# Later result stores, an earlier embedding load, two additions on VectorE and another order of weight pieces in the last stage of a hybrid decoder layer

## The chip, the cores and the metric

The kernel runs on one core of a Trainium2 chip. Five engines work side by side, each with its own instruction stream: TensorE (PE in the profile; PEld are its weight loads), VectorE (DVE), ScalarE (ACT), GpSimd (POOL) and SyncE (SP). SP and ACT issue the DMAs of this kernel; "SPq" and "ACTq" mark such an issue. An engine takes its instructions in order, so an instruction that waits holds up all that stand behind it. The metric is the device time of one execution, in microseconds; less is better.

## The reference

One layer of a decoder, in float32, for 2048 prompt tokens and 64 sample tokens of width 1024:

```python
proj = xn @ w_in + b_in
...
y_a = (o * jax.nn.silu(za)) @ w_br_a
...
y_b = (cv * jax.nn.silu(zb)) @ w_br_b
merged = jax.nn.sigmoid(ma) * y_a + jax.nn.sigmoid(mb) * y_b
h = h + merged @ w_o
gate = jax.nn.sigmoid(_rmsnorm(h, norm_ple) @ w_ple_gate)
h = h + gate * (p_l @ w_ple)
...
y_prompt = _rmsnorm(hp, norm_final)
```

The recurrence behind `o` and the convolution behind `cv` stand ahead of the part that is changed. Only the last four statements matter here.

## The kernel before

Stages 1 and 2 (projections, recurrence, convolution, both branches, `merged`) take the first 2320 us or so of the profiled execution and write `merged` to DRAM as `mg_dr`. The change is all in stage 3, the last 490 us.

Every float32 operand of a product is split into a high part (a ScalarE copy that rounds) and a low part (what VectorE or GpSimd then subtracts), and a product is the sum of three TensorE products (high by high, high by low, low by high). Stage 3 takes 256 rows at a time, a *pair* of two 128-row blocks, r = 0 and 1. A pair's 256x1024 by 1024x1024 product is done with seven products of half size in place of eight; each is twelve matmuls into one PSUM tile of 128x512. Left operands are quarters of the input (`a11`, `a12`, `a22`) or sums of quarters (`s1` to `s4`, made on GpSimd at L1281, tile `sf`). Their splits are L1288 (ScalarE) and L1289 (VectorE), tiles `l_a` and `l_s`. Right operands are quarters of the weight (`b11`, `b12`, `b21`, `b22`) or their differences (`t1` to `t4`, in DRAM as `ts_dr`).

Sixteen stages of the loop run one after the other, each with seven products i = 0 to 6. Pairs 0 to 7 are the **first pass**: `h = x + merged @ w_o`. After products 0, 1 and 3 the method `more` adds a running sum to a half row block of `h` (GpSimd, L1331), `close` adds a product from PSUM (VectorE, L1335) and squares it (ScalarE, L1383), `scale` stores `h` to `h_dr` (L1346) and scales it by its norm, and `turn` transposes it into `t_dr` (L1398 to L1403). Pairs 8 to 15 are the **gate pass**: the same seven products on `t_dr` with `w_ple_gate`, plus four small products `pp` (L1428) of the embeddings with `w_ple`. The embeddings `p` are loaded (L1300) and transposed (`turn_p`: tile `pt`, L1415; split at L1417 and L1418 into `x1h` and `x1l`). `gate_sum` (L1360, L1361) and `gate_use` (L1366, L1367) put the gate on; `finish` scales by the final norm (VectorE, L1376) and stores the result from ScalarE's queue (L1377).

The order is written out by hand. The loop issues product i of pair n, then the pair's own VectorE and ScalarE work, then `prepare` (sums and splits for the next pair), and then what `at_step(n, i, fn)` has put behind that product. `finish(1)` of a pair comes after its product 6, `finish(0)` after product 0 of the next pair. Row tiles `h` have three buffers, so that the load of a later block (L1294, SP's queue) waits for the store of an earlier one. The gate pass needs other right operands than the first pass. Sixteen 256 KB pieces of them go during pairs 7 and 8 through three buffers (`bwr`, L1605; splits at L1608 and L1609), `t1` and `t4` come whole (1 MB each, L1639, tile `x0l`, splits at L1645 and L1646), and `w_ple` comes in four pieces during pair 5. At the start of stage 3 the pieces of `b22` (for the last product of pair 0) take the same way.

Sample rows are a small extra product in pairs 3 and 11.

Of the kernel before, what the change touches and what calls it, by code (L numbers as in the profile page):

```python
# [86 lines left out]
def f32(ap):  # L87
    return ap.bitcast(F32)
# [3 lines left out]
def tile_hybrid_step(  # L92
# [1152 lines left out]
    class Pair:  # L1245
# [81 lines left out]
            nc.scalar.activation(out=self.u["p1"], in_=self.ps[0], func=AF.Copy)  # L1327


        def more(self, r, e, t):  # L1330
            nc.gpsimd.tensor_tensor(out=self.part(r, e), in0=self.part(r, e), in1=t, op=ALU.add)  # L1331

        def close(self, r, e, d):
            h = self.part(r, e)
# [35 lines left out]
        def finish(self, r):  # L1370
            b = 2 * self.i + r
            rs = rstd(self.ss[r], P)
            for e in range(2) if (self.i, r) == (7, 0) else (None,):
                c = slice(0, D) if e is None else slice(G * e, G * (e + 1))
                h = self.h[r][:, c]
                nc.vector.scalar_tensor_tensor(out=h, in0=h, scalar=rs, in1=fin["n"][:, c], op0=ALU.mult, op1=ALU.mult)  # L1376
                nc.scalar.dma_start(out=y_p[0, b * P:(b + 1) * P, c], in_=h)  # L1377

    def square(h, out, junk=None):
        n = h.shape[0]  # L1380
# [51 lines left out]
    class Sample:  # L1432
# [72 lines left out]
        def finish(self):  # L1505
            rs = rstd(self.ss, NS)
            nc.vector.scalar_tensor_tensor(
                out=self.h[0:NS], in0=self.h[0:NS], scalar=rs, in1=fin["n"][0:NS], op0=ALU.mult, op1=ALU.mult)
            nc.scalar.dma_start(out=y_s2, in_=self.h[0:NS])

    pairs = [[Pair(i, g) for i in range(8)] for g in range(2)]
    samples = [Sample(g) for g in range(2)]
# [116 lines left out]
    def right_load(w, op):  # L1629

        right_new(op)
        lo = right[op][1]
        if op in QUARTERS:
            r, c = QUARTERS[op]
            src = (w_o, w_ple_gate)[w][0][G * r:G * (r + 1), G * c:G * (c + 1)]
        else:
            r0 = (4 * w + int(op[1]) - 1) * G
            src = ts_dr[r0:r0 + G]
        nc.sync.dma_start(out=f32(lo), in_=src.rearrange("(k p) c -> p k c", p=P))  # L1639

    def right_split(op):
        hi, lo = right[op]
# [17 lines left out]
    def first_pass(q, i):  # L1660
        if i == 0:
            q.keep_p1()
            q.more(0, 0, q.u["p1"])
        elif i == 1:
            q.more(0, 1, q.sum_u(1, "p1", "u2"))
        elif i == 2:
            q.close(0, 0, 2)
        elif i == 3:
            t = q.sum_u(3, "u2", "u3")
            q.more(1, 1, t)  # L1670
            q.more(1, 0, t)
        elif i == 4:
            q.close(1, 1, 4)
            h = q.part(0, 1)
            nc.vector.tensor_tensor(out=h, in0=q.ps[4], in1=h, op=ALU.add)
        elif i == 5:
            q.close(1, 0, 5)
        else:
            q.scale(1)
            q.close(0, 1, 6)  # L1680
# [28 lines left out]
    for n, q in enumerate(stages):  # L1709
        nxt = stages[n + 1] if n < 15 else None  # L1710
        if n < 14:
            at_step(n, 6, stages[n + 2].load_raw)
        if nxt:
            at_step(n + 1, 1, lambda q=nxt: q.split("s4"))
            at_step(n, 3, lambda q=nxt: q.load_h(1))
            at_step(n, 6, lambda q=nxt: q.load_h(0))
        if n < 8:
            at_step(n + 1, 1, lambda q=q: q.turn(1))
            at_step(n + 1, 3, lambda q=q: q.turn(0))
        else:  # L1720
            at_step(n - 1, 4, q.load_p)
            at_step(n, 0, lambda q=q: q.turn_p(0))
            at_step(n, 1, lambda q=q: q.turn_p(1))
            if n < 15:
                at_step(n + 1, 0, lambda q=q: q.finish(0))
# [15 lines left out]
            at_step(7, i + 1, lambda op=op, k=k: piece_split(op, k))  # L1741
    for i, op in ((5, "t1"), (5, "t4")):
        at_step(7, i, lambda op=op: right_load(1, op))
    for i, op in ((7, "t1"), (8, "t4")):
        at_step(7, i, lambda op=op: right_split(op))
    for i, fn in ((6, lambda: b22_load(1, 0, 1, 2)), (7, lambda: b22_split(0)), (7, lambda: b22_load(1, 3)),
                  (8, lambda: b22_split(1, 2)), (8, lambda: b22_split(3))):
        at_step(7, i, fn)
    for k in range(2):
        for e in range(2):  # L1750
            c, i = slice(G * e, G * (e + 1)), 2 * k + e
            at_step(5, i, lambda k=k, c=c, i=i: late_load(("p", i), w_ple[0][P * k:P * (k + 1), c]))
            at_step(5, i + 3, lambda k=k, c=c, i=i: late_split(("p", i), wph[:, k, c], wpl[:, k, c]))
    fin = {}

    def load_fin():
# [2 lines left out]

    at_step(8, 0, load_fin)  # L1760

    stages[1].load_raw()
    b22_load(0, 0, 1, 2)
    stages[0].load_h(1)
    stages[0].load_h(0)
    stages[0].split("s1")
# [2 lines left out]
    stages[0].add("s4")  # L1769
    stages[0].split("a22")  # L1770
    at_step(0, 0, lambda: stages[0].split("s4"))
    at_step(0, 3, lambda: b22_split(0, 1, 2))
    at_step(0, 3, lambda: b22_load(0, 3))
    at_step(0, 4, lambda: b22_split(3))
    for n, q in enumerate(stages):
        smp = samples[n // 8] if n % 8 == 3 else None
        nxt = stages[n + 1] if n < 15 else None
        for i in range(7):
# [4 lines left out]
            if smp and i == 5:  # L1783
                smp.split()
                nxt.split("s2")
            elif nxt:
                prepare(nxt, i)
            if q.gate:
                second_use(q, i)
# [3 lines left out]
                smp.ph = turn_ple(smp.p, NS, 0)  # L1793
            for fn in extra.get(7 * n + i, ()):
                fn()
        if smp:
            for e in range(2):
                (smp.gated if smp.gate else smp.out_proj)(e)
# [3 lines left out]
            else:  # L1802
                at_step(n + 1, 3, smp.scale)
                at_step(n + 1, 5, smp.turn)
    stages[15].finish(0)


_INS = ['x_prompt', 'x_sample', 'state_hgrn', 'state_conv', 'p_prompt', 'p_sample', 'lb_param', 'norm_mix', 'w_in',
# [26 lines left out]
```

## Time and profile before

| | us |
|---|---|
| median of three runs | 2815.18 (2815.08 to 2815.82) |
| the profiled execution's own time | 2815.05 |
| its span in the trace | 2813.3 |
| TensorE busy | 2721.9 (97%) |
| VectorE busy | 2049.3 (73%) |
| ScalarE busy | 997.1 (35%) |
| GpSimd busy | 463.6 (16%) |

The span runs from the first to the last instruction of the trace; the 1.75 us between it and the execution's own time lie around it. The busy shares are means over the whole span. The change is in the last sixth of it, so what counts there are the waits of that stretch: which instruction TensorE waited for, for how long, and what that instruction had waited for.

### The profile page before, as it was taken

How to read it: one execution, taken by the hardware profiler on the slowest of the kernel's cores; microseconds unless marked ns; L12 is line 12 of the kernel's file. 1: busy time of each engine (PE TensorE's matmuls, PEld its weight loads, DVE VectorE, ACT ScalarE, POOL GpSimd, SP SyncE). 2: the span in 40 equal slices, each digit the busy share in tenths (PEclk: the TensorE clock that was granted, in tenths of full speed). 3: DMA queues.
4: the chain of work that ended last, by engine and by line, in shares of the span. 5: the costliest groups of instructions: out<-in, count | busy, mean ns of one | idle time of the engine just before them, and what ended most of it. 6: DMA issues, size and time to landing. Idle time of an engine off the chain costs nothing.

```text
span 2813.3 us, 51106 instructions
## 1 busy us (share of the span) xinstructions
PE 2721.9 (97%) x21063; PEld 2335.1 (83%) x21063; DVE 2049.3 (73%) x3308; ACT 997.1 (35%) x2243; POOL 463.6 (16%) x573
## 2 busy tenths in 40 slices
PE   8999999999999999999999999999999999986997
PEld 6888888888888889989989999898898897765776
DVE  6677777876878787777787868789778655455665
ACT  5333333333332432333332333324244324454332
POOL 2000000000000010101011010101155304453221
PEclk9999999999999999999999999999999999998999
DMA  3212223222221422322222322325877785565321
GB/s 123 71 61 83 76 83 98 76 83 65 83 65 56 139 88 75 104 86 92 79 92 82 99 86 80 101 90 182 260 219 244 223 257 188 160 211 187 113 101 71
DMA packets 354162, 333.09 MB, mean 118 GB/s; under 512 B 20794, under 2 KB 286107, under 8 KB 353928
## 3 DMA queue, kind: packets, MB, share of 16 engines
q1 hardware_dynamic: 279120, 224.43, 26.2%
q10 hardware_dynamic: 74536, 105.20, 10.7%
q8 instruction: 165, 2.70, 0.4%
q14 instruction: 69, 0.57, 0.1%
q0 software_dynamic: 272, 0.19, 0.0%
HBM read 224.58 MB, written 105.18 MB: 117 GB/s over the span
## 4 chain that ended last, share of the span: by engine, by line
PE 81%; DVE 6%; ACT 3%; POOL 3%; issue 2%; DMA 2%; ACTq 0%; SPq 0%; POOLq 0%; DVEq 0%
PE mm L1583 69%; PE ps L1312 2%; PE d32p L504 1%; PE ab L512 1%; DVE acc L756 1%; POOL sf L1281 1%; PE o L602 1%; PE kv L575 1%; PE o L604 1%; DVE h L1367 1%; POOL h L1331 1%; PE pp L1428 1%; ACT l_s L1288 1%; DVE h L1376 1%; DMA h_dr<-h 1%
## 5 line engine op out<-in xcount | busy, mean ns | idle before, releaser
L756 DVE SCALAR_TENSOR_TENSOR acc<-u,cw,acc 128x512 f32<-128x512 f32 x960 | 742.9, 774 | 20.7
L1583 PE MATMUL mm<-x1h,whi 128*128 128x320 f32 (+2 forms) x2112 | 706.6, 335 | 0.0
L1583 PE MATMUL mm<-x1h,wlo 128*128 128x320 f32 (+2 forms) x2112 | 689.2, 326 | 0.0
L1583 PE MATMUL mm<-x1l,whi 128*128 128x320 f32 (+2 forms) x2112 | 689.1, 326 | 0.0
L1583 PE MATMUL mm<-x0h,whi 128*128 128x512 f32 (+1 forms) x1416 | 562.5, 397 | 0.0
L1583 PE MATMUL mm<-x0l,whi 128*128 128x512 f32 (+1 forms) x1416 | 551.3, 389 | 2.5 <-DVE x0l L203 2.5
L1583 PE MATMUL mm<-x0h,wlo 128*128 128x512 f32 (+1 forms) x1416 | 551.4, 389 | 0.3 <-DVE wlo L364 0.3
L1583 PEld LDWEIGHTS mm<-x1h,whi 128*128 128x128 f32 x2112 | 398.0, 188 | 30.9 <-issue 1.9
L1583 PEld LDWEIGHTS mm<-x1h,wlo 128*128 128x128 f32 x2112 | 398.2, 189 | 28.2
L1583 PEld LDWEIGHTS mm<-x1l,whi 128*128 128x128 f32 x2112 | 398.0, 188 | 26.2
L364 DVE TENSOR_TENSOR wlo<-raw,whi 128x1024 fp32r<-128x1024 f32 x176 | 218.4, 1241 | 208.7 <-ACT whi L360 202.6
L1583 PEld LDWEIGHTS mm<-x0h,wlo 128*128 128x128 f32 x1416 | 266.2, 188 | 57.6 <-DVE wlo L364 1.2
L1583 PEld LDWEIGHTS mm<-x0h,whi 128*128 128x128 f32 x1416 | 266.8, 188 | 53.7 <-issue 1.2
L1583 PEld LDWEIGHTS mm<-x0l,whi 128*128 128x128 f32 x1416 | 266.7, 188 | 53.7 <-DVE x0l L203 3.2
L613 POOL TENSOR_SCALAR ors<-oss 128x4 f32<-128x4 f32 (+1 forms) x40 | 12.2, 305 | 1341.8 <-ACT on L611 1341.8
L360 ACT ACTIVATE whi<-raw 128x1024 fp32r<-128x1024 f32 x176 | 186.2, 1058 | 101.7 <-DVE mal L951 35.0
L465 DVE TENSOR_TENSOR rp<-rp 128x512 f32<-128x512 f32 (+1 forms) x224 | 156.7, 699 | 9.9 <-DVE lvl L478 0.5
L478 DVE TENSOR_TENSOR lvl<-kq,rp 128x512 f32<-128x512 f32 (+2 forms) x224 | 150.7, 673 | 1.9
L839 ACT ACTIVATE sp<-mm,vcol 128x512 f32<-128x512 f32 (+2 forms) x120 | 73.0, 609 | 127.4 <-PE mm L1583 115.1
L1312 PE MATMUL ps<-r_t,l_s 128*128 128x512 f32 x384 | 106.4, 429 | 6.8 <-ACT l_s L1288 6.8
L1312 PEld LDWEIGHTS ps<-r_t,l_s 128*128 128x128 f32 x384 | 79.1, 210 | 29.2 <-ACT l_s L1288 9.0
L721 ACT ACTIVATE sg<-mm,vcol 128x512 f32<-128x512 f32 (+2 forms) x40 | 24.6, 614 | 203.4 <-PE mm L1583 163.9
(297 smaller groups left out, 3530.2 us busy)
## 6 DMA issues: line engine op xcount, KB each, us to landing
raw<-in_w_in_dram SPq DMA_DIRECT2D x144, 512.0 KB, 3.9
gate<-am_dr SPq DMA_DIRECT2D x24, 512.0 KB, 5.0
xt<-in_x_prompt_dram SPq DMA_DIRECT2D x16, 512.0 KB, 5.0
g_dr<-gst ACTq DMA_DIRECT2D x32, 256.0 KB, 2.9
cv_dr<-acc ACTq DMA_DIRECT2D x32, 256.0 KB, 2.0
ts_dr<-ts ACTq DMA_DIRECT2D x32, 256.0 KB, 4.3
raw<-in_w_br_a_dram SPq DMA_DIRECT2D x16, 512.0 KB, 4.9
raw<-in_w_br_b_dram SPq DMA_DIRECT2D x16, 512.0 KB, 6.5
```

The source lines that it names most:

```text
L360: nc.scalar.activation(out=b.hi, in_=b.raw, func=AF.Copy)
L364: nc.vector.tensor_tensor(out=b.lo, in0=b.raw, in1=f32(b.hi), op=ALU.subtract)
L465: nc.vector.tensor_tensor(out=io, in0=io, in1=tt, op=ALU.mult)
L478: nc.vector.tensor_tensor(out=o, in0=a, in1=b, op=ALU.mult)
L504: nc.tensor.matmul(dst[32 * b:32 * b + 32, c, s:s + 16], lhsT=kk[:, o:o + 32], rhs=lv[:, o:o + 32].rearrange("p (a e i) -> p a e i", e=2, ...
L512: nc.tensor.matmul(self.ab[o:o + h, c, o + h:o + 2 * h], lhsT=lv[:, P * c + o:P * c + o + h], rhs=lv[:, P * c + o + h:P * c + o + 2 * h], ...
L575: nc.tensor.matmul(self.kv[:, c, :], lhsT=self.kt[:, c, :], rhs=self.v[:, c, :], start=True, stop=True)
L602: nc.tensor.matmul(self.o[:, c, :], lhsT=at[:, c, :], rhs=self.v[:, c, :], start=True, stop=last)
L756: nc.vector.scalar_tensor_tensor(out=self.acc, in0=self.u[:, i:i + G], scalar=w, in1=self.acc, op0=ALU.mult, op1=ALU.add)
L839: nc.scalar.activation(out=s[:, 0:n], in_=ps[:, 0:n], func=func, bias=bias(kind, j))
L1312: nc.tensor.matmul(ps, lhsT=a[:, k, :], rhs=b[:, k, :], start=(k == 0 and j == 0), stop=(k == 3 and j == 2))
L1583: nc.tensor.matmul(ps[:, 0:u.n], lhsT=w[:, k, :], rhs=x[:, k, sl], start=(k == 0 and w is u.block.hi and x is xh), stop=(k == KB - 1 and w ...
```

## The change

All edits are in stage 3.

- The stores of `y` are no longer issued where `finish` computes them. They are put into a list and issued two products later (`y_store`, `y_flush`); what is left is issued at the end.
- The embeddings of pair 8, the first of the gate pass, are loaded after product 0 of pair 6 instead of product 4 of pair 7. Later pairs keep their place.
- After product 3 of a first-pass pair, the two additions `more(1, 1)` and `more(1, 0)` go to VectorE instead of GpSimd.
- `t1` and `t4` of the gate weight are loaded from ScalarE's queue instead of SP's, and each is split one product later. The pieces of `b22` of the gate weight are loaded one or two products earlier, their splits are grouped otherwise.
- The pieces of `w_ple` are still loaded in pair 5 (the last one in pair 6), but split in pair 6.
- At the start, the pieces of `b22` are loaded ahead of pair 1's input and split after product 1 instead of 3; the split of pair 1's `a11` moves from product 0 to product 2.

```diff
-        def more(self, r, e, t):
-            nc.gpsimd.tensor_tensor(out=self.part(r, e), in0=self.part(r, e), in1=t, op=ALU.add)
+        def more(self, r, e, t, engine=nc.gpsimd):
+            engine.tensor_tensor(out=self.part(r, e), in0=self.part(r, e), in1=t, op=ALU.add)
...
-                nc.scalar.dma_start(out=y_p[0, b * P:(b + 1) * P, c], in_=h)
+                y_store(y_p[0, b * P:(b + 1) * P, c], h)
+
+    step = [0]
+    due = []
+
+    def y_store(out, in_):
+
+        due.append((step[0] + 2, out, in_))
+
+    def y_flush():
+        while due and due[0][0] <= step[0]:
+            _, out, in_ = due.pop(0)
+            nc.scalar.dma_start(out=out, in_=in_)
...
-        nc.sync.dma_start(out=f32(lo), in_=src.rearrange("(k p) c -> p k c", p=P))
+        nc.scalar.dma_start(out=f32(lo), in_=src.rearrange("(k p) c -> p k c", p=P))
...
-            q.more(1, 1, t)
-            q.more(1, 0, t)
+            q.more(1, 1, t, nc.vector)
+            q.more(1, 0, t, nc.vector)
...
-            at_step(n - 1, 4, q.load_p)
+            at_step(n - 1 if n > 8 else 6, 4 if n > 8 else 0, q.load_p)
...
-    for i, op in ((7, "t1"), (8, "t4")):
+    for i, op in ((8, "t1"), (9, "t4")):
         at_step(7, i, lambda op=op: right_split(op))
-    for i, fn in ((6, lambda: b22_load(1, 0, 1, 2)), (7, lambda: b22_split(0)), (7, lambda: b22_load(1, 3)),
-                  (8, lambda: b22_split(1, 2)), (8, lambda: b22_split(3))):
+    for i, fn in ((5, lambda: b22_load(1, 0, 1)), (6, lambda: b22_load(1, 2)), (7, lambda: b22_split(0, 1)),
+                  (7, lambda: b22_load(1, 3)), (8, lambda: b22_split(2, 3))):
         at_step(7, i, fn)
...
+    for i, (t0, t1) in enumerate(((0, 8), (1, 9), (2, 10), (9, 13))):
+        k, e = i // 2, i % 2
+        c = slice(G * e, G * (e + 1))
+        at_step(5, t0, lambda k=k, c=c, i=i: late_load(("p", i), w_ple[0][P * k:P * (k + 1), c]))
+        at_step(5, t1, lambda k=k, c=c, i=i: late_split(("p", i), wph[:, k, c], wpl[:, k, c]))
...
+    b22_load(0, 0, 1, 2)
     stages[1].load_raw()
-    b22_load(0, 0, 1, 2)
...
-    at_step(0, 3, lambda: b22_split(0, 1, 2))
-    at_step(0, 3, lambda: b22_load(0, 3))
-    at_step(0, 4, lambda: b22_split(3))
+    at_step(0, 1, lambda: b22_split(0, 1, 2))
+    at_step(0, 1, lambda: b22_load(0, 3))
+    at_step(0, 2, lambda: stages[1].split("a11"))
+    at_step(0, 3, lambda: b22_split(3))
...
-            elif nxt:
+            elif nxt and (n or i):
                 prepare(nxt, i)
...
+            y_flush()
+            step[0] += 1
```

ScalarE, from the square after product 5 of pair 14 to the gate of product 2 of pair 15, before. `g,ss<-h` at L1383 is the square, `p` the copy of product 0, `x1h` the splits of the embeddings' transposes, `out_dram` the stores of `y`:

```order
L1383 ACTIVATE g,ss<-h 128x512
L1377 DMA out_dram<-h 128x1024
L1361 ACTIVATE g<-g 128x512
L1288 ACTIVATE l_s_26823<-sf 128x512
L1383 ACTIVATE g,ss<-h 128x512
L1327 ACTIVATE p_26846<-ps 128x512
L1377 DMA out_dram<-h 128x1024
L1417 ACTIVATE x1h<-pt 128x256
L1288 ACTIVATE l_s_26874<-sf 128x512
L1417 ACTIVATE x1h<-pt 128x256
L1361 ACTIVATE g<-g 128x512
```

The same stretch now (the lines of the file have moved by 12: L1389 is the store, L1395 the square, L1429 the split):

```order
L1395 ACTIVATE g,ss<-h 128x512
L1361 ACTIVATE g<-g 128x512
L1288 ACTIVATE l_s_26822<-sf 128x512
L1395 ACTIVATE g,ss<-h 128x512
L1327 ACTIVATE p_26845<-ps 128x512
L1429 ACTIVATE x1h<-pt 128x256
L1288 ACTIVATE l_s_26872<-sf 128x512
L1429 ACTIVATE x1h<-pt 128x256
L1389 DMA out_dram<-h 128x1024
L1361 ACTIVATE g<-g 128x512
L1395 ACTIVATE g,ss<-h 128x512
L1389 DMA out_dram<-h 128x1024
```

Both stores have moved behind both splits; the store of block 1 from ahead of product 6's gate to behind the second split, the store of block 0 behind the next square.

GpSimd in pair 0 of the first pass, from the second `more` on, before and now. `h<-h,u` are the `more` additions, `sf` the sums for the next pair, `rs` the three steps of a norm:

```order
L1331 TENSOR_TENSOR h<-h,u_23431 128x512
L1331 TENSOR_TENSOR h<-h,u_23467 128x512 x2
L1281 TENSOR_TENSOR sf<-mgr 128x512 x2
L1281 TENSOR_TENSOR sf<-sf,mgr 128x512
L1387 TENSOR_TENSOR rs_23545<-ss 128x1
```

```order
L1331 TENSOR_TENSOR h<-h,u_23428 128x512
L1281 TENSOR_TENSOR sf<-mgr 128x512 x2
L1281 TENSOR_TENSOR sf<-sf,mgr 128x512
L1399 TENSOR_TENSOR rs_23545<-ss 128x1
L1400 TENSOR_SCALAR rs_23545<-rs_23545 128x1
```

The two additions are gone from GpSimd; they stand in VectorE's stream right behind the sum `u` of product 3.

ScalarE from product 5 of pair 7 into pair 8, before. `r_t` are pieces of gate weights, `x0l` and `x0h` the parts of `t1` and `t4`, `x1h<-bwr` the pieces of `b22`:

```order
L1608 ACTIVATE r_t_25100<-bwr 128x512 x3
L1346 DMA h_dr<-h 128x1024
L1383 ACTIVATE junk,ss<-h 128x512
L1288 ACTIVATE l_s_25164<-sf 128x512
L1608 ACTIVATE r_t_25100<-bwr 128x512
L1346 DMA h_dr<-h 128x1024
L1327 ACTIVATE p_25203<-ps 128x512
L1288 ACTIVATE l_a_25205<-mgr 128x512
L1417 ACTIVATE x1h<-pt 128x256
L1645 ACTIVATE x0h<-x0l 128x512 x4
L1608 ACTIVATE x1h<-bwr 128x512
```

The same stretch now:

```order
L1620 ACTIVATE r_t_25100<-bwr 128x512 x3
L1651 DMA x0l<-ts_dr 128x4x512 x2
L1346 DMA h_dr<-h 128x1024
L1395 ACTIVATE junk,ss<-h 128x512
L1288 ACTIVATE l_s_25168<-sf 128x512
L1620 ACTIVATE r_t_25100<-bwr 128x512
L1346 DMA h_dr<-h 128x1024
L1327 ACTIVATE p_25203<-ps 128x512
L1288 ACTIVATE l_a_25205<-mgr 128x512
L1429 ACTIVATE x1h<-pt 128x256
L1620 ACTIVATE x1h<-bwr 128x512 x2
```

The two loads `x0l` are new in this stream, ahead of both stores to `h_dr`; the splits of `x0l` have left this place for a later product.

## Rows read from the trace of the kernel before

**Rows 1.** The page: the busy time of each engine in us (share of the span) and its instructions.

```profile
PE 2721.9 (97%) x21063; PEld 2335.1 (83%) x21063; DVE 2049.3 (73%) x3308; ACT 997.1 (35%) x2243; POOL 463.6 (16%) x573
```

**Rows 2.** The waits of TensorE in stage 3 (2320 to 2814 us): the waiting operation, what released it, then us in total, how many times, the longest.

```profile
PE pp L1428 <- ACT x1h L1417: 33.6, 8, 8.8
PE pt L1415 <- DMA p<-in_p_prompt_dram: 8.7, 1, 8.7
PE ps L1312 <- ACT l_s L1288: 6.8, 5, 3.3
PE ps L1312 <- ACT x1h L1608: 2.8, 2, 1.5
```

**Rows 3.** The chain that ended last, at the step from pair 12 to pair 13 of the gate pass: start, length, what.

```profile
2723.32 0.53 ACT l_a L1288
...
2724.48 1.29 DVE h L1376
2725.79 0.34 ACTq L1377
...
2728.28 7.08 PE ps L1312 x24
...
2756.78 1.66 PE pp L1428 x6
```

**Rows 4.** The timelines of PE, DVE and ACT at the same place: start, length, engine, line, operation, tiles, and in brackets the idle time before it and what ended it.

```profile
2726.61 0.50 PE L1428 MATMUL pp<-x1h 128*128 128x512 f32 x1 [3.23 <-ACT x1h L1417]
...
2727.18 0.40 PE L1428 MATMUL pp<-x1h,x1l 128*128 128x512 f32 x1
...
2726.59 0.42 DVE L1418 TENSOR_TENSOR x1l<-pt,x1h 128x256 fp32r<-128x256 f32 x1 [0.83 <-ACT x1h L1417]
...
2731.75 0.69 DVE L1367 TENSOR_TENSOR h<-g,h 128x512 f32<-128x512 f32 x1
...
2726.98 0.38 ACT L1417 ACTIVATE x1h<-pt 128x256 fp32r<-128x256 f32 x1
```

**Rows 5.** Busy time of each engine in two stretches of 30 us of the gate pass, then the granted clock as a share of full speed, the DMA share and GB/s.

```profile
2715.00:2745.00 30.00, 26.77 (x113) 21.48 (x112) 18.64 (x26) 9.98 (x22) 7.38 (x10) 0.94 0.32 114
2745.00:2775.00 30.00, 26.77 (x120) 21.72 (x119) 18.56 (x27) 10.38 (x24) 8.34 (x13) 1.00 0.23 79
```

**Rows 6.** DMA issues from 2716 to 2735 us (first two rows) and from 2535 to 2565 us (the others): count, KB each, median us from issue to landing.

```profile
out_dram<-h ACTq DMA_DIRECT2D x2, 512.0 KB, 2.6
h<-h_dr SPq DMA_DIRECT2D x2, 512.0 KB, 3.3
...
x0l<-ts_dr SPq DMA_DIRECT2D x2, 1024.0 KB, 10.3
mgr<-t_dr SPq DMA_DIRECT2D x4, 512.0 KB, 11.2
...
h<-h_dr SPq DMA_DIRECT2D x2, 512.0 KB, 7.0
```

**Rows 7.** The start of stage 3, timelines of PE (the last product of pair 0, then products 0 and 1 of pair 1) and DVE.

```profile
2341.25 0.50 PE L1312 MATMUL ps<-x1h,l_s 128*128 128x512 f32 x1 [1.50 <-ACT x1h L1608]
2342.66 0.80 PE L1312 MATMUL ps<-x1l,l_s 128*128 128x512 f32 x1 [0.90 <-DVE x1l L1609]
...
2350.38 3.99 PE L1312 MATMUL ps<-r_b,l_a 128*128 128x512 f32 x12
2354.21 1.98 PE L1312 MATMUL ps<-r_t,l_s 128*128 128x512 f32 x8
...
2341.92 4.05 DVE L1609 TENSOR_TENSOR x1l<-bwr,x1h 128x512 fp32r<-128x512 f32 x3
...
2352.50 0.69 DVE L1289 TENSOR_TENSOR l_s<-sf,l_s 128x512 fp32r<-128x512 f32 x1 [2.59 <-ACT l_s L1288]
```

**Rows 8.** The chain that ended last in the first pass, pairs 1 and 2: start, length, what.

```profile
2374.43 2.61 DMA h_dr<-h
...
2388.54 2.54 POOL h L1331 x2
...
2396.58 2.61 DMA h_dr<-h
```

**Rows 9.** Pairs 5 and 6 of the first pass: PE from product 0 of pair 6 on, and DVE on two of the pieces of `w_ple`.

```profile
2471.52 2.88 PE L1312 MATMUL ps<-r_b,l_a 128*128 128x512 f32 x12
2477.74 4.86 PE L1312 MATMUL ps<-r_t,l_s 128*128 128x512 f32 x12 [3.33 <-ACT l_s L1288]
2482.44 1.03 PE L1398 MATMUL pt<-ident,hs 128*128 128x128 f32 x8
2483.23 0.96 PE L1312 MATMUL ps<-r_b,l_a 128*128 128x512 f32 x3
...
2469.93 1.36 DVE L1609 TENSOR_TENSOR x1l<-bwr,x1h 128x512 fp32r<-128x512 f32 x1 [1.81 <-ACT x1h L1608]
...
2473.87 0.68 DVE L1609 TENSOR_TENSOR x1l<-bwr,x1h 128x512 fp32r<-128x512 f32 x1
```

**Rows 10.** From pair 7 to pair 8: the timelines of PE and ACT.

```profile
2533.59 4.66 PE L1312 MATMUL ps<-r_t,l_s 128*128 128x512 f32 x12 [1.58 <-ACT l_s L1288]
2552.59 0.80 PE L1428 MATMUL pp<-x1h 128*128 128x512 f32 x1 [6.20 <-ACT x1h L1417]
...
2551.64 0.63 ACT L1288 ACTIVATE l_a<-mgr 128x512 fp32r<-128x512 f32 x1 [7.80 <-DMA mgr<-t_dr]
```

More of the change, by code (lines that the diff above doesn't have):

```diff
@@ L1508, in finish @@
                 out=self.h[0:NS], in0=self.h[0:NS], scalar=rs, in1=fin["n"][0:NS], op0=ALU.mult, op1=ALU.mult)
-            nc.scalar.dma_start(out=y_s2, in_=self.h[0:NS])
+            y_store(y_s2, self.h[0:NS])
     pairs = [[Pair(i, g) for i in range(8)] for g in range(2)]
@@ L1743, in tile_hybrid_step @@
         at_step(7, i, lambda op=op: right_load(1, op))
-    for i, op in ((7, "t1"), (8, "t4")):
+    for i, op in ((8, "t1"), (9, "t4")):
         at_step(7, i, lambda op=op: right_split(op))
-    for i, fn in ((6, lambda: b22_load(1, 0, 1, 2)), (7, lambda: b22_split(0)), (7, lambda: b22_load(1, 3)),
-                  (8, lambda: b22_split(1, 2)), (8, lambda: b22_split(3))):
+    for i, fn in ((5, lambda: b22_load(1, 0, 1)), (6, lambda: b22_load(1, 2)), (7, lambda: b22_split(0, 1)),
+                  (7, lambda: b22_load(1, 3)), (8, lambda: b22_split(2, 3))):
         at_step(7, i, fn)
[L1749 to L1753, printed above, removed]
+    for i, (t0, t1) in enumerate(((0, 8), (1, 9), (2, 10), (9, 13))):
[3 more added lines that the diff above has]
+        at_step(5, t1, lambda k=k, c=c, i=i: late_split(("p", i), wph[:, k, c], wpl[:, k, c]))
     fin = {}
@@ L1804, in tile_hybrid_step @@
                 at_step(n + 1, 5, smp.turn)
+    step[0] += 9
+    y_flush()
     stages[15].finish(0)
+    step[0] += 9
+    y_flush()
 _INS = ['x_prompt', 'x_sample', 'state_hgrn', 'state_conv', 'p_prompt', 'p_sample', 'lb_param', 'norm_mix', 'w_in',
```

## The prediction

> **What bounds the kernel now.** The page first: TensorE is busy for 97% of the span [rows 1], so a gain must come out of the time in which it stands still or runs slowly. The view of waits, cut to stage 3, says where it stands still [rows 2]: 33.6 us in eight waits for the split `x1h` of the embeddings, 8.7 in one wait for the first load of `p`, 6.8 for operand splits, 2.8 for the splits of `b22`.
>
> The chain of waits shows why the largest recurs [rows 3]. Where one gate pair follows another it runs through VectorE's final scaling (2724.48, 1.29 us), ScalarE's issue of the store (2725.79) and the split `x1h`, and TensorE restarts at 2726.61 after 3.23 us of idleness [rows 4]. The split needs nothing of the scaling. It stands behind the store in ScalarE's stream, and the store waits for the scaled tile. The next such restart is at 2756.78 [rows 3], 30.17 us later.
>
> The idleness costs twice. Twelve matmuls take 2.88 us where nothing slows them [rows 9]; less the 0.40 of one [rows 4] that is 2.48 for eleven starts, 0.226 apart, so 24 need 5.4. Behind the restart 24 take 7.08 [rows 3], 1.6 more. The stretches say what it is: the granted clock is 0.94 from 2715 to 2745, and 1.00 from 2745 to 2775, which holds the restart at 2756.78 [rows 5]. So TensorE falls to the lower of its two levels (1.2 and 2.4 GHz) behind a restart, though not behind each.
>
> In the first pass the chain runs through GpSimd: `more` for 2.54 us, and later the store of `h`, at 2374.43 and again at 2396.58 [rows 8], 22.15 us apart. TensorE needs 84 matmuls at 0.226 (19.0 us) and two groups of transposes (2482.44 to 2483.23 [rows 9], 0.8 each), 20.6 in all. So this loop leads, not TensorE.
>
> **Part 1, the stores of y.** Without the store `x1h` starts when ScalarE is done with `l_a`, 2723.32 + 0.53 = 2723.85 [rows 3], and ends 0.38 later [rows 4]. Two `pp` matmuls can go; the third reads the low part `x1l`, which VectorE makes behind its scaling, and VectorE's order is as before. The scaling ends at 2725.77, `x1l` takes 0.42 [rows 4], so the third matmul comes at about 2726.25 instead of 2727.18: 0.9 gained. TensorE is then idle in two pieces of about 0.9 and 1.5 us instead of one of 3.23. Whether the clock falls after such a pair is not shown in this order. At the start of the stage pieces of 1.50 and 0.90 are followed by a matmul of 0.80 [rows 7], the lower level; behind the restart at 2756.78 nothing fell. I take half of the 1.6, hence 0.9 + 0.9 = 1.8 per restart, and six restarts of this form (pairs 10 to 15): 10.8 us. Bounds: 6 x 0.9 less 6 x 0.4 (below) is 3; 6 x 2.5 and 1 at pair 9 is 16.
>
> The price is the row tile. Block 0 of the next pair is loaded into the tile that block 1's store reads. That store now stands behind the second split, which ends at 2727.36 [rows 4] and some 2 us sooner without the first store, so it goes at 2725.2; it lands 2.6 later, and the load needs 3.3 more [rows 6], so the tile is there at about 2731.2. Its reader L1367 stands at 2731.75 [rows 4], 0.9 earlier now: 2730.85. Queued behind it on VectorE is the pair's next work, which waits for products of TensorE; those cover the 0.4 us, and without that cover it is 0.4 per pair. At the end the last stores leave later: 0.3 us lost.
>
> **Part 2, two additions on VectorE.** GpSimd loses 2.54 us per pair [rows 8]; VectorE gains two additions of 0.69 (like L1367 [rows 4]). Net 1.2 per pair, of the 1.5 that TensorE allows. It counts where the loop leads, in three pairs ahead of pair 3's sample rows: 3.6 us. Bounds 0 and 5 x 1.5 = 7.5.
>
> The row to weigh is a subtraction of the same size, also with two inputs in SBUF: 0.68 at 2473.87, but 1.36 at 2469.93 [rows 9]. A pair that costs 2 x 1.36 leaves no gain against 2.54, which is the lower bound above. The Trainium skill (SBUF — State Buffer, "SBUF: two separate sides") states that VectorE with two inputs in SBUF and GpSimd lock each other out of a shared port pair for a whole instruction. By that rule, if one addition of each two meets a sum of GpSimd, the term is 3 x 0.5 = 1.5 instead of 3.6. The two durations agree with it.
>
> **Part 3, the pieces of w_ple.** Their four splits leave the vector streams of pair 5, behind which TensorE waited 3.33 us and ran 12 matmuls in 4.86 instead of 2.88 [rows 9]: up to 5.3 us. They come back in pair 6 with 4 x 0.68 on VectorE, nearly all on pair 7's chain: 2.5 of wait and 1.4 of lower clock given back. Net 1.4; bounds -1 and 5.
>
> **Part 4, the start.** The last product of pair 0 waits 1.50 and 0.90 for the `b22` splits and runs slowly until 2350.38 [rows 7]. With three splits two products earlier it can begin when the product before it ends (2341.25 - 1.50 = 2339.75) and needs 2.7 us; the fourth piece is still loaded only when a buffer is free, for which I add 2: it ends near 2344.4. Then the vector chain is late next: product 1 of pair 1 needs `l_s`, which VectorE begins at 2352.50. In that chain stood three splits of `b22`, 4.05 us [rows 7]; they go ahead of it, the two new additions (1.4) come in, so 2.6 are gained, and product 1 starts at about 2350.2 instead of 2354.21: 4 us. Bounds 1 (the splits hold up the first closing instead) and 6.
>
> **Part 5, pair 7 to pair 8.** Product 1 of pair 8 starts at 2533.59, released by `l_s` and not by `p` [rows 10]. So the earlier load of `p`, for all its 8.7 us among the waits, gains nothing by itself. What can gain is `mgr`, for which ScalarE waits 7.80 us until 2551.64, with the next `x1h` behind it and TensorE idle for 6.20 [rows 10]. On SP's queue it stood behind 2 x 1024 KB of `t1` and `t4`, and took 11.2 us [rows 6]. Those are on the other queue now. Between 11.2 and the 3.3 of a tile of the same size elsewhere [rows 6] I take the middle, 7.3: some 4 us sooner, to which 1 to 2 of clock come. Against that: the stores to `h_dr` now stand behind `t1` and `t4`, which take 10.3; the loads of `h` and the last pieces of `b22` on SP wait for them, and `t4` is split a product later. I take 2 off, so +3.5, between 8 (all of `mgr`'s 8) and -3 (nothing for `mgr`, and the stores 3 later).
>
> In that stretch a load of `h` takes 7.0 instead of 3.3 [rows 6], so more of one queue is less of the other. The Trainium skill (DMA: Bandwidth & Descriptors, "Queues, rings and completion order") says that an engine takes turns between the rings that have work, packet by packet. By that rule `mgr` would have half of the rate and land about 5 us sooner; no row here shows two full queues.
>
> **The sum.** 10.8 - 0.3 + 3.6 + 1.4 + 4 + 3.5 = 23.0 us off the profiled execution's 2815.05, which is 0.13 below the median of the runs. Forecast: 2792 us.
>
> **Rivals.**
> A, the forecast. Its own range is 2783 to 2802.
> B, order alone: the clock still falls behind each restart, and pair 7 to 8 gains nothing since it is bound by its sixteen pieces. 4 + 3 + 6 x 0.9 = 12.4: 2803. For it: the 0.80 us matmul behind two short pauses [rows 7]. Against it: a stretch without a fall behind 3.23 [rows 5].
> C, all of the clock and more at pair 7 to 8: 4 + 5 + 8 + 6 x 2.5 = 32, and 5 more if `mgr` and part 3 reach their upper bounds: 2778 to 2783. For it, the exception of rows 5; against it, pair 8's two late operands at once.
> D, slower: the row tile. If the load of `h` takes L instead of 3.3 us, it comes L - 2.95 after its reader is ready, and a gate pair takes 30.17 - 0.9 + L - 2.95. With the 7.0 of the crowded stretch [rows 6] a pair is 3.1 longer; seven pairs make 22, against 12.5 gained elsewhere: 2825. It decides from L = 5.6 on. For it: the load now follows right behind a store, with `mgr` close. Against it: the DMA share of the gate pass is 0.23 to 0.32 [rows 5].
> E, no change: VectorE's work from L1367 to the next scaling is the loop, and each matmul that comes sooner waits longer at the next restart. 2812 to 2818. Against it: the chain passes through 24 matmuls of TensorE in each pair [rows 3].
>
> **Chances.** A 0.55, B 0.25, C 0.08, D 0.06, E 0.06. Faster by over 0.2% (5.6 us, about what a measurement of this kernel can tell from no change) are A, B and C, 0.88; E gives 0.06 for the same, D 0.06 for slower. The range that holds the time 8 times in 10 takes A, B and most of C: 2778 to 2808.
>
> **What would show it.** In the changed kernel's waits of TensorE, `pp` on `x1h` should go from 33.6 to under 10, with `x1l` as a new releaser; the gate restarts should lie about 28.4 apart, with a granted clock of 1.00 in half of the stretches. Product 1 of pair 1 should start near 2350, and ScalarE's wait for `mgr` be under 4 us. A clock of 0.94 in every stretch would show B, VectorE waiting at L1367 for the DMA of `h` D, an unchanged 30.17 E. What would make it wrong by most is a new wait in pairs 7 and 8, where sixteen pieces share three buffers and the order of the loads is new.

## The result and the profile after

The changed kernel takes 2790.49 us (median of three runs, 2789.93 to 2794.97) against 2815.18: a ratio of 0.9916 with a 95% interval of 0.9894 to 0.9939, 24.7 us faster. Timed again in five rounds it took 2795.39 (2795.16 to 2797.32) against 2816.29: 0.9929 (0.9915 to 0.9942), 20.9 us. The forecast was 2792.

The waits of TensorE from 2300 us on in the changed kernel, in the columns of [rows 2] (L1440 is `pp`, L1429 and L1430 are the splits of the embeddings; the lines have moved by 12):

```profile
PE ps L1312 <- ACT l_s L1288: 16.5, 3, 11.2
PE pp L1440 <- ACT x1h L1429: 12.9, 8, 4.4
PE pp L1440 <- DVE x1l L1430: 8.9, 7, 1.3
PE ps L1312 <- ACT x0h L1657: 5.6, 1, 5.6
```

`pp` on `x1h` has gone from 33.6 to 12.9 us (the prediction had under 10), and `x1l` is its new second releaser, 1.3 us at each of seven restarts. The wait for `p` has gone, but `l_s` has grown from 6.8 to 16.5, with one piece of 11.2. That is the same stop at product 1 of pair 8 under another name. The 5.6 us for `x0h` (the split of `t4`) are new.

One restart of the gate pass (the place in each pair where TensorE goes on with the first `pp`) on PE, beside which [rows 4] stands for before:

```profile
2607.68 0.50 PE L1440 MATMUL pp<-x1h 128*128 128x512 f32 x1 [0.78 <-ACT x1h L1429]
2608.01 0.40 PE L1440 MATMUL pp<-x1l,x1h 128*128 128x512 f32 x1
2609.66 0.50 PE L1440 MATMUL pp<-x1h,x1l 128*128 128x512 f32 x1 [1.25 <-DVE x1l L1430]
2610.00 0.39 PE L1440 MATMUL pp<-x1h 128*128 128x512 f32 x1
```

The idle time of 3.2 us has become 0.78 and 1.25, as part 1 had it (0.9 and 1.5), and the matmuls behind it run at 0.39, the higher clock. The sections of stage 3 show the clock at large. Before, then after; columns as in [rows 5] (the last three are granted clock, DMA share, GB/s). The first row of each is the first pass from product 1 of pair 1 to product 1 of pair 7, the second pair 7's product 1 to pair 8's, the third from there to product 3 of pair 9, the fourth the gate pass to the last product of pair 15:

```profile
2354.00:2501.00 147.00, 139.07 (x650) 112.99 (x648) 73.17 (x105) 74.10 (x209) 76.94 (x86) 0.99 0.58 183
2501.00:2534.00 33.00, 22.47 (x103) 17.97 (x104) 19.53 (x23) 19.22 (x46) 20.20 (x19) 0.89 0.63 207
2534.00:2598.00 64.00, 43.58 (x161) 33.56 (x161) 37.81 (x48) 28.18 (x65) 22.36 (x25) 0.82 0.51 181
2598.00:2800.00 202.00, 183.38 (x777) 147.68 (x775) 128.75 (x181) 66.91 (x147) 44.42 (x63) 0.96 0.29 101
```

```profile
2348.00:2490.00 142.00, 137.28 (x649) 113.41 (x648) 83.37 (x119) 73.89 (x210) 61.27 (x76) 0.99 0.61 194
2490.00:2523.00 33.00, 21.84 (x103) 17.70 (x103) 22.14 (x26) 18.86 (x46) 17.66 (x16) 0.89 0.59 199
2523.00:2582.00 59.00, 42.14 (x160) 32.44 (x160) 34.07 (x48) 28.00 (x64) 20.84 (x25) 0.85 0.54 187
2582.00:2776.00 194.00, 180.10 (x779) 144.22 (x779) 129.06 (x182) 66.54 (x147) 45.26 (x63) 0.99 0.31 108
```

The same matmuls take 8 us less in the gate pass, at 0.99 instead of 0.96 of the clock. The first pass is 5 us shorter (3 in the second trace of the changed kernel, see below), with VectorE busy for 10 us more and GpSimd for 16 less. Pair 7 to 8 has not moved, and the section behind it is 5 us shorter.

### The profile page after: what moved, and what is told of

Its sections match the earlier page's. It is cut to its first block, busy times and chain, and to the rows that moved or that the text cites. A ratio compares the mean times of both kernels' runs of the same rounds, so it can differ in the third digit from the quotient of the medians.

```text
span 2788.7 us, 51107 instructions
## 1 busy us (share of the span) xinstructions
PE 2709.7 (97%) x21063; PEld 2328.9 (84%) x21063; DVE 2054.8 (74%) x3324; ACT 996.4 (36%) x2243; POOL 440.3 (16%) x557
## 3 DMA queue, kind: packets, MB, share of 16 engines
q1 hardware_dynamic: 278064, 222.33, 26.3%
## 5 line engine op out<-in xcount | busy, mean ns | idle before, releaser
L1595 PEld LDWEIGHTS mm<-x1l,whi 128*128 128x128 f32 x2112 | 397.7, 188 | 26.3
L1312 PE MATMUL ps<-r_t,l_s 128*128 128x512 f32 x384 | 100.1, 411 | 16.5 <-ACT l_s L1288 16.5
```

The source lines that it names most:

```text
L1312: nc.tensor.matmul(ps, lhsT=a[:, k, :], rhs=b[:, k, :], start=(k == 0 and j == 0), stop=(k == 3 and j == 2))
L1595: nc.tensor.matmul(ps[:, 0:u.n], lhsT=w[:, k, :], rhs=x[:, k, sl], start=(k == 0 and w is u.block.hi and x is xh), stop=(k == KB - 1 and w ...
```

## The experiments

All but the first timing of the changed kernel, above, ran in five rounds beside the kernel before, and each left one trace. The table gives the ratio with its interval, and from the PE timeline of each trace the length of five sections of stage 3 in us: **a** from its first product to product 1 of pair 1, **b** to product 1 of pair 7, **c** to product 1 of pair 8, **d** to product 3 of pair 9, **e** to the last product of pair 15.

| kernel | ratio (95%) | a | b | c | d | e |
|---|---|---|---|---|---|---|
| before | 1 | 31.0 | 147.1 | 32.3 | 64.2 | 202.4 |
| changed | 0.9916 (0.9894 to 0.9939) | 25.9 | 142.1 | 32.8 | 59.6 | 193.5 |
| changed, once more | 0.9929 (0.9915 to 0.9942) | 25.8 | 143.8 | 32.5 | 60.6 | 194.5 |
| stores at once | 0.9957 (0.9945 to 0.9970) | 27.0 | 144.2 | 32.9 | 61.5 | 201.8 |
| before, stores later only | 0.9965 (0.9953 to 0.9978) | 29.9 | 149.0 | 32.0 | 61.8 | 193.4 |
| additions on GpSimd | 0.9955 (0.9941 to 0.9969) | 26.5 | 152.0 | 33.1 | 59.8 | 192.7 |
| before, additions on VectorE only | 0.9967 (0.9955 to 0.9980) | 29.6 | 141.7 | 32.1 | 63.1 | 200.8 |
| w_ple as before | 0.9922 (0.9909 to 0.9934) | 25.8 | 143.8 | 32.6 | 59.3 | 192.3 |
| start as before | 0.9926 (0.9913 to 0.9939) | 29.2 | 144.0 | 32.4 | 60.1 | 192.2 |
| t1, t4 on SP's queue | 0.9928 (0.9914 to 0.9942) | 26.1 | 144.4 | 32.3 | 60.8 | 193.9 |
| p late | 0.9926 (0.9914 to 0.9939) | 26.3 | 143.7 | 34.0 | 60.4 | 195.1 |
| stores one product later | 0.9940 (0.9928 to 0.9953) | 26.2 | 144.4 | 32.8 | 59.2 | 195.5 |
| x1l ahead of the scaling | 0.9901 (0.9887 to 0.9915) | 27.0 | 143.7 | 31.9 | 57.7 | 188.3 |
| that, and t4 split earlier | 0.9917 (0.9903 to 0.9930) | 25.5 | 144.9 | 33.6 | 58.2 | 190.5 |

A section's length varies between traces of the same instructions: **e** is 192.2 to 195.1 in the eight traces that share the changed kernel's gate pass (mean 193.4), and 200.8 to 202.4 in the three with the stores at once; **b** is 147.1 and 149.0 in two kernels that are alike there. A difference of 2 us in one section is therefore no finding by itself.

**The stores.** At once again in the changed kernel:

```diff
-        due.append((step[0] + 2, out, in_))
+        nc.scalar.dma_start(out=out, in_=in_)
```

> The changed kernel with the stores of y issued at once again, all else as changed. Theory (the stores ahead of x1h are what made the gate restarts late, and the idle time of 3.2 us is what lowered the clock): the gate pass loses what the traces give it, 9 us from the first restart of pair 9 to the end, so about 2799 to 2801; single idle pieces of about 3.2 us ahead of pp are back, restarts about 30 us apart, and the granted clock falls behind most of them. Rival (the order of the stores is worth only the 0.9 us by which the third pp matmul comes sooner; the rest came from pairs 7 and 8 being out of the way): 6 x 0.9, so about 2796, with the granted clock as in the changed kernel.

Measured 2804.28 us. Section e is back at 201.8 and the clock is back at 0.94 in three of its stretches. In the waits of TensorE `x1h` is back at 27.6 us, and `x1l` is not among them:

```profile
PE pp L1440 <- ACT x1h L1429: 27.6, 8, 5.9
PE ps L1312 <- ACT l_s L1288: 17.1, 5, 11.2
```

```profile
2620.00:2650.00 30.00, 26.81 (x113) 21.55 (x112) 18.92 (x27) 11.22 (x24) 7.63 (x11) 0.94 0.45 145
2680.00:2710.00 30.00, 27.08 (x114) 21.82 (x113) 20.17 (x28) 11.19 (x24) 6.54 (x9) 0.94 0.30 103
2710.00:2740.00 30.00, 26.81 (x114) 21.51 (x113) 18.58 (x26) 10.12 (x22) 7.36 (x10) 0.94 0.32 112
```

Single idle pieces of 2.8 to 3.2 us stand ahead of the six restarts from pair 10 on again, and the clock fell behind four of them. The theory holds, with 3 us more than it had, 1 to 2 of them in section d; the rival's 2796 does not. The kernel before with the later stores alone (`y_store` and `y_flush` as in the change, nothing else):

> The kernel before with only the stores of y two products later. Theory (the parts add up): 9 us less than before, about 2806, all of it behind pair 9's restart. Rival (the gain in the gate pass needs the other edits, since a late pair 8 leaves the weight splits in its way): 4 us or less, 2811 or more.

Measured 2807.16, with e at 193.4, as in the changed kernel: the theory holds here too. The waits of TensorE keep those of before's first pass and of pairs 7 and 8, 8.1 us for `p` among them:

```profile
PE pp L1440 <- ACT x1h L1429: 18.3, 8, 6.9
PE pt L1427 <- DMA p<-in_p_prompt_dram: 8.1, 1, 8.1
PE pp L1440 <- DVE x1l L1430: 7.9, 7, 1.3
```

So the later stores are worth some 8 us in section e, with the other edits and without them.

**The additions.** Back on GpSimd in the changed kernel:

```diff
-            q.more(1, 1, t, nc.vector)
-            q.more(1, 0, t, nc.vector)
+            q.more(1, 1, t)
+            q.more(1, 0, t)
```

> The changed kernel with the two additions back on GpSimd. Theory from the two traces (between product 1 of pair 1 and the sample rows the change gained 1.3 us): 1 to 2 us slower, about 2792. Rival, the term as it stood in the prediction (1.2 us in each of three pairs): 3.6 us slower, about 2794. Second rival (VectorE's additions beside GpSimd's sums cost as much as they free): no change, 2790.5.

Measured 2802.02, beyond every expectation. Section b takes 152.0, 8 to 10 us more than in the changed kernel and 5 more than before: the early start is given back too. PE at product 1 of pairs 6 and 7, and GpSimd's additions in pair 6:

```profile
2476.32 3.30 PE L1312 MATMUL ps<-r_t,l_s 128*128 128x512 f32 x12 [2.53 <-ACT l_s L1288]
2501.69 2.71 PE L1312 MATMUL ps<-r_t,l_s 128*128 128x512 f32 x6 [3.96 <-ACT l_s L1288]
...
2492.55 2.54 POOL L1331 TENSOR_TENSOR h<-h,u 128x512 f32<-128x512 f32 x2 [4.43 <-DMA h<-in_x_prompt_dram]
```

The wait ahead of product 1 of pair 6 is there although no piece of `w_ple` is split in pair 5. (The second row shows the first six of the product's twelve matmuls.) The additions alone on the kernel before, whose pair 5 still has all four splits:

> The kernel before with only the two additions on VectorE. Theory from the run that undid them (its trace ends 11.5 us behind the changed kernel's, 3.5 of them up to the sample rows and 6 more by product 1 of pair 7): the first-pass loop is where the time is, so they are worth 6 to 10 us alone, 2806 to 2810. Rival (they pay only where the w_ple splits have left pair 5 and stand in pair 6; alone it is the 3.6 us of the prediction): about 2812. Second rival (pairs 7 and 8, bound by their weight pieces, take up all of it): 2815.

Measured 2806.81, 9.9 us less than before: the theory holds, and the prediction's 3.6 falls. Section b is 5.4 us shorter: 1.3 of it between product 1 of pair 1 and that of pair 3, 4.0 between those of pairs 5 and 7. The other 4.3 us of this trace lie in the four other sections, at most 1.6 in each. PE at product 1 of pair 6, which [rows 9] has at 2477.74 behind 3.33 us and at the lower clock:

```profile
2473.48 3.30 PE L1312 MATMUL ps<-r_t,l_s 128*128 128x512 f32 x12 [0.41 <-ACT l_s L1288]
```

Twelve matmuls in 3.30 instead of 4.86, behind 0.41: the additions by themselves take that wait away.

**The pieces of w_ple** as before, in the changed kernel:

```diff
-    for i, (t0, t1) in enumerate(((0, 8), (1, 9), (2, 10), (9, 13))):
...
+    for k in range(2):
+        for e in range(2):
+            c, i = slice(G * e, G * (e + 1)), 2 * k + e
+            at_step(5, i, lambda k=k, c=c, i=i: late_load(("p", i), w_ple[0][P * k:P * (k + 1), c]))
+            at_step(5, i + 3, lambda k=k, c=c, i=i: late_split(("p", i), wph[:, k, c], wpl[:, k, c]))
```

> The changed kernel with the pieces of w_ple loaded and split in pair 5 as before. Theory from the traces (5.5 us gained up to pair 6, 2.2 given back at product 1 of pair 7): 3 us slower, about 2794, with a wait of l_s of about 3 us ahead of product 1 of pair 6 and none ahead of that of pair 7. Rival, the term of the prediction: 1.4 us slower. Second rival (pairs 7 and 8 are bound by their sixteen pieces, which take up whatever pair 6 gains): no change.

Measured 2794.57; b is 143.8, as in the second trace of the changed kernel. My theory from the traces was wrong, and no change, the time of the second rival, is what came. PE at product 1 of pairs 6 and 7 in this run, then in the changed kernel's second trace, shows why:

```profile
2470.54 3.30 PE L1312 MATMUL ps<-r_t,l_s 128*128 128x512 f32 x12 [0.58 <-ACT l_s L1288]
2493.12 3.30 PE L1312 MATMUL ps<-r_t,l_s 128*128 128x512 f32 x12 [0.69 <-ACT l_s L1288]
```

```profile
2468.95 2.89 PE L1312 MATMUL ps<-r_t,l_s 128*128 128x512 f32 x12
2492.87 4.36 PE L1312 MATMUL ps<-r_t,l_s 128*128 128x512 f32 x12 [2.94 <-ACT l_s L1288]
```

With the additions on VectorE the splits in pair 5 cost only 0.58 us ahead of pair 6; split in pair 6 they cost 2 us more ahead of pair 7. Between product 1 of pairs 5 and 7 the two orders differ by 0.5 us (44.2 and 44.7).

**The start** as before (`b22` loaded behind pair 1's input and split after product 3, `a11` after product 0):

> The changed kernel with the start of stage 3 as before (loads and splits of b22, split of a11). Theory (with the additions on VectorE TensorE leads in the first pass, so a late start is carried to the end): 3 to 5 us slower, 2794 to 2796. Rival (the vector loop or the weight pieces of pairs 7 and 8 take it up): no change, about 2791.

Measured 2795.91. Section a is 3.4 us longer (29.2 against 25.8), as the theory had it, and b and c + d are as in the changed kernel's second trace, so the start is still late at pair 9. But e, in which nothing differs, is 192.2 against 194.5, and from the first product of stage 3 to the end of the span this trace has 470.8 us, the two of the changed kernel 470.3 and 466.9. The gain is there at its place and is not taken up by the first pass; what it is worth at the end, between 0.5 and 3.9 us, is within the scatter of e and stays open.

**The queue of t1 and t4**, back on SP:

```diff
-        nc.scalar.dma_start(out=f32(lo), in_=src.rearrange("(k p) c -> p k c", p=P))
+        nc.sync.dma_start(out=f32(lo), in_=src.rearrange("(k p) c -> p k c", p=P))
```

> The changed kernel with t1 and t4 loaded from SP's queue again. Theory, the term of the prediction: mgr then lands 4 us or so later, ScalarE waits for it for 8 to 10 us instead of 6.0, and it is 3 us slower, about 2794. Rival (the DMA engines are full in that stretch, so that another queue only changes who is late, and h_dr's stores gain what mgr loses): no change, about 2791.

Measured 2796.87, ratio 0.9928, as the changed kernel's second timing. ScalarE does wait longer for `mgr`, 8.7 us instead of 6.0, the row of this kernel ahead of that of the changed one:

```profile
ACT l_a L1288 <- DMA mgr<-t_dr: 8.7, 1, 8.7
```

```profile
ACT l_a L1288 <- DMA mgr<-t_dr: 6.0, 1, 6.0
```

Yet c and d together take 93.1 against 92.4 and 93.1 in the two traces of the changed kernel. The rows of `h_dr` and `mgr` at the step from pair 7 to 8, of this kernel and then of the changed one (second trace), from issue to landing, say why:

```profile
h_dr<-h ACTq DMA_DIRECT2D x2, 512.0 KB, 8.1
mgr<-t_dr SPq DMA_DIRECT2D x2, 512.0 KB, 12.2
```

```profile
h_dr<-h ACTq DMA_DIRECT2D x2, 512.0 KB, 13.2
mgr<-t_dr SPq DMA_DIRECT2D x2, 512.0 KB, 10.3
```

The DMA share is 0.93 to 0.95 there in both. The rival holds: `mgr` gains 1.9 us by the other queue and the stores to `h_dr` lose 5.1.

**The load of p**, late again:

```diff
-            at_step(n - 1 if n > 8 else 6, 4 if n > 8 else 0, q.load_p)
+            at_step(n - 1, 4, q.load_p)
```

> The changed kernel with the embeddings of pair 8 loaded behind product 4 of pair 7 again. Theory, as in the prediction (product 1 of pair 8 waits for l_s at about 2522.6, 11 us behind the transposes of p): the load may land up to 11 us later at no cost; same time, with the wait split into one for p and one for l_s. Rival (the transposes and their wait are on the path, as the 8.7 us in the waits of the kernel before suggest, and the load again crowds the weight pieces): 2 to 8 us slower.

Measured 2794.42 against 2795.39 for the changed kernel on the same chip. The wait splits in two, as expected:

```profile
PE pt L1427 <- DMA p<-in_p_prompt_dram: 9.6, 1, 9.6
...
PE ps L1312 <- ACT l_s L1288: 7.7, 4, 2.8
```

An entry of 9.6 us in the list of waits was worth nothing that the timing shows. Section c is 1.2 to 1.5 longer here; whether that is the load's doing stays open.

**The changed kernel once more, and stores one product later** (`step[0] + 1` in place of `step[0] + 2`):

> The changed kernel once more, unedited, so that the others are read beside it on the same chip. It should repeat 2790.5 within 2 us. Its trace tells how much of the differences between traces is chance: the start of stage 3 has come between 2321.8 and 2326.6 us in kernels whose code is the same up to there, and the clock behind the sample rows of pair 3 fell in some traces and not in others.

It took 2795.39, not 2790.5, and its gain is 20.9 us instead of 24.7.

> The changed kernel with the stores of y one product later instead of two. Theory (what counts is that no store that waits for the final scaling stands ahead of x1h in ScalarE's stream): block 0's store still stands behind both splits, so the time is the changed kernel's, about 2790.5, and the gaps ahead of the gate restarts are the same 0.8 and 1.25. Rival (the distance itself counts, since a store that is issued sooner crowds the load of the next row tile): 2 to 4 us slower.

Measured 2800.50 (2796.47 to 2800.71). The gaps at the restarts are the same 0.78 and 1.25, e is 1 us longer, of which 0.7 is a wait for the sample rows' embeddings, and the stretch from the first product of stage 3 to the end is 0.8 longer. The 5 us between the medians are not in the traces (the traced execution, 2797.92, is one of the two quick ones of five; the others took 2800.5 to 2800.7), and the intervals of the two ratios overlap. Whether one product costs something stays open.

**Beyond the change.** The split of the embeddings ahead of the scaling:

```diff
-            at_step(n, 0, lambda q=q: q.turn_p(0))
+            extra.setdefault(7 * n, []).insert(0, lambda q=q: q.turn_p(0))
```

> The changed kernel with one more edit: the split of the embeddings is put ahead of the final scaling of the previous pair in VectorE's stream (the transposes of block 0 are placed first behind product 0). Theory (the third pp matmul waits 1.25 us for x1l only because the scaling of 1.28 us stands ahead of it): this idle time goes at seven restarts, 7 to 9 us faster than the changed kernel, about 2782. Rival (VectorE's chain is the loop of the gate pass, and the scaling that moves behind costs as much later in the pair): less than 2 us, about 2790.

Measured 2788.50, the lowest ratio of all, 0.9901. Its interval overlaps those of the changed kernel, so the time alone does not show a gain, but e is 188.3, against 192.2 to 195.5 in every other kernel with later stores (the last one below shares this edit). PE at the same restart as above:

```profile
2609.98 0.50 PE L1440 MATMUL pp<-x1h 128*128 128x512 f32 x1 [0.76 <-ACT x1h L1429]
2610.32 0.40 PE L1440 MATMUL pp<-x1l,x1h 128*128 128x512 f32 x1
2610.77 0.50 PE L1440 MATMUL pp<-x1h,x1l 128*128 128x512 f32 x1
```

The second piece of idle time is gone, and some 5 us of the expected 7 to 9 came of it in section e. At three restarts the wait for `x1h` has grown instead: by 0.6 us at pairs 11 and 15 and by 1.2 at pair 13 (3.46 instead of 2.27). With the split of `t4` one product earlier (`(8, "t4")` in place of `(9, "t4")`) as well:

> The changed kernel with the split of the embeddings ahead of the final scaling and the split of t4 one product earlier (behind product 1 of pair 8, together with t1's). Theory (in the changed kernel TensorE waits 5.6 us in pair 8 because t4's split stands behind a square on ScalarE that waits for the gate): 3 to 5 us faster than with the embeddings' split alone, and 6 to 8 faster than the changed kernel, about 2783 to 2785. Rival (t1's and t4's splits together hold up the gate of product 2, and the wait moves there): the same as with the embeddings' split alone, 2788.

Measured 2792.65, and e is 190.5. The 5.6 us for `x0h` went, and came back as four others on PE (the last was 2.28 with the embeddings' split alone):

```profile
2559.54 0.50 PE L1440 MATMUL pp<-x1h 128*128 128x512 f32 x1 [0.89 <-DVE g L1360]
2562.05 0.50 PE L1440 MATMUL pp<-x1h 128*128 128x512 f32 x1 [0.84 <-DVE g L1366]
2571.64 4.87 PE L1312 MATMUL ps<-r_t,l_s 128*128 128x512 f32 x12 [2.26 <-ACT l_s L1288]
2583.98 0.80 PE L1440 MATMUL pp<-x1h 128*128 128x512 f32 x1 [4.52 <-ACT x1h L1429]
```

The theory does not hold; the wait moves, as the rival had it, and the 4 us above the rival's 2788 are not explained. Pairs 7 to 9 are bound by something that this split does not shorten; what it is was not found.

## Why the prediction was right, and which steps were not

The total came out within 2 us of the first timing and 3.4 of the second, but not by its own terms, and that it did is luck: part 2 measured 6 us more than it had, and what the other parts measured less makes up for it. The two edits that earn it are the stores (9.5 us alone) and the additions (9.9 us alone): 19.4 of the 20.9 to 24.7. Undoing the order of `w_ple`, the start, the queue of `t1` and `t4` or the load of `p`, each alone, gave ratios of 0.9922 to 0.9928, between the changed kernel's own two, 0.9916 and 0.9929. One edit was never undone by itself: the later splits of `t1` and `t4` and the new order of the gate weight's `b22` (pieces 0 and 1 are loaded one product earlier, the other two where they were).

- Part 1, 10.8 us: right in kind, and near in size (8 in section e, 9.5 alone). Of its two halves the clock did better than taken: at the five restarts with idle pieces of at most 0.8 and 1.35 the clock stayed at the higher level; it fell at the two with 3.19 and 2.27 ahead of 1.25. The restarts of pairs 10 and 11 lie 27.6 us apart (2609.66 to 2637.22), those of pairs 13 and 14, with the lower clock between them, 29.2 (2706.02 to 2735.22). The other traces bear this out, though not without exception. From pair 10 on the clock fell behind 13 of 18 restarts in the three kernels with the stores at once, and behind 9 of 54 in the nine traces with later stores and the old split order: six at pair 13, where `x1h` was 2.2 to 2.6 us late, and three at pair 12 behind pieces of only 0.5 and 1.25, such as this one with the additions on GpSimd (twelve matmuls in 4.14 us; they take 2.9 at the higher clock):

```profile
2689.68 0.50 PE L1440 MATMUL pp<-x1h,x1l 128*128 128x512 f32 x1 [1.25 <-DVE x1l L1430]
...
2691.08 4.14 PE L1312 MATMUL ps<-r_t,l_s 128*128 128x512 f32 x12
```

  Short pieces made a fall rarer and did not rule it out. With the stores at once and no fall pairs 10 and 11 lie 28.5 us apart, so the order is worth the 0.9 that the prediction had; a fall adds 1.6. (By the prediction's own spacing 24 matmuls need 5.6 us and not 5.4; the difference is too small to matter.) The term of 0.3 us for the last stores was nothing: from the start of the last product to the end there are 13.05 us before and 13.04 after.
- The price of the row tile, 0.4 us: not there. The rows of the changed kernel at the restart of pair 13, ACT, SP and DVE:

```profile
2701.99 0.63 ACT L1395 ACTIVATE g<-h 128x512 f32<-128x512 f32 x1 [2.67 <-DVE h L1367]
2702.01 0.34 ACTq L1389 DMA_DIRECT2D out_dram<-h  x1
2702.62 0.58 ACT L1327 ACTIVATE p<-ps 128x512 f32<-128x512 f32 x1
...
2703.61 0.37 ACT L1429 ACTIVATE x1h<-pt 128x256 fp32r<-128x256 f32 x1
...
2704.40 0.38 ACT L1429 ACTIVATE x1h<-pt 128x256 fp32r<-128x256 f32 x1
...
2704.68 0.32 SPq L1294 DMA_DIRECT2D h<-h_dr  x1
...
2710.70 0.69 DVE L1367 TENSOR_TENSOR h<-g,h 128x512 f32<-128x512 f32 x1
```

  The store left at 2702.01, not behind the second split at 2704.78, and the load was issued at 2704.68; with 3.3 us to landing it was there 2.8 us ahead of its reader, which did not wait. Rival D has the same store 3 us too late.
- Part 2, 3.6 us: the step that failed. "It counts where the loop leads, in three pairs ahead of pair 3's sample rows": there the run with the additions alone has 1.3, and 4.0 between pairs 5 and 7, where the sum's next term looked for them. Measured: 5.4 us in section b when done alone, 8 to 10 there when undone in the changed kernel, 9.9 in all. What an addition costs on VectorE shows on DVE in pairs 5 and 7 of the changed kernel (two additions to a row), with GpSimd's work beside the second:

```profile
2457.85 1.29 DVE L1331 TENSOR_TENSOR h<-h,u 128x512 f32<-128x512 f32 x2
...
2509.15 2.77 DVE L1331 TENSOR_TENSOR h<-h,u 128x512 f32<-128x512 f32 x2
...
2508.03 1.64 POOL L1621 TENSOR_TENSOR r_t<-bwr,r_t 128x512 fp32r<-128x512 f32 x1
2509.63 1.74 POOL L1281 TENSOR_TENSOR sf<-mgr 128x512 f32<-128x512 f32 x1
```

  In pair 5, where GpSimd has nothing to do, they cost what the sum had, in pair 7, beside GpSimd's work, twice that. The Trainium skill (SBUF — State Buffer, "SBUF: two separate sides") has VectorE with two inputs in SBUF and GpSimd shut each other out of a shared port pair. The trace agrees with it in pair 7. Both sums for part 2, the prediction's and the one by that rule, were too small.
- Part 3, 1.4 us: its 5.3 us belonged to part 2. The waits at pair 6 were put down to the splits of `w_ple` because those stood in the streams there; the run that moved only the additions took the wait away with the splits in place, and moving the splits on top of it was worth nothing (0.9922 without, 0.9916 and 0.9929 with).
- Part 4, 4 us: 3.4 to 5 at its place (section a; product 1 of pair 1 at 2347.67), but between 0.5 and 3.9 from the start of the stage to its end when undone alone, which the scatter of section e hides. With the additions on GpSimd section b takes it back whole, so it needs part 2, which the prediction did not say. (Its own rows give 2350.6 and not 2350.2 for product 1, 3.6 us and not 4.)
- Part 5, 3.5 us: sections c and d are 3.4 to 4.1 shorter in sum, of which the later stores bring 2.7 alone (32.0 and 61.8) and the additions alone 1.4 (32.1 and 63.1), so hardly anything is left for the edits of this part. The queue moved ScalarE's wait for `mgr` by 2.7 us and the time by nothing; that wait was 6.0, not under 4. That the load of `p` gains nothing was right.
- B is not what happened (the clock stayed up behind most restarts), nor E: section e shrank by 8.

## What to carry to other kernels

An instruction that waits, like a store for its tile, stands in the way of all that is behind it on its engine; putting it behind the work that TensorE needs gave some 8 us, part of it through the clock. Cost an edit by undoing it and by doing it alone before a wait is put down to what happens to stand near it: here two additions closed a gap that four splits were blamed for. And an entry in a list of waits is worth only the distance to the next operand that is late, which for `p` was nothing that could be measured.

## What the runs showed that was not expected

ScalarE's stores leave ahead of work that stands before them in its stream: the issue at 2702.01 came 1.6 us before the first and 2.4 before the second split that precede it in the order. It came 0.02 us behind the start of the square (2701.99), the last instruction ahead of it that had waited for another engine; 14 of the 16 stores between 2570 and 2783 us left within 0.03 us of such a square. So a DMA need not wait until the arithmetic ahead of it on its engine has run, where the operands of that arithmetic are there; in the kernel before it was the other way round, and the store, waiting for its tile, held up the splits behind it. How far a store can run ahead was not tried.

The first product of stage 3 came between 2321.8 and 2326.6 us in kernels whose instructions are the same up to there, and the clock at the sample rows of pair 3 stayed up in one trace of the changed kernel (1.00 from 2405 to 2440) and fell in the other (0.95), whose section b is 1.7 longer. So two traces of one kernel differ by 4.8 us of span (2788.7 and 2793.5), and a difference of that size between two kernels has to be found in a section before it means anything.
